# A decoder layer's opening: products of un-normed x, norms made beside them, and ten products of a constant ahead of all

## The chip, the cores and the metric

One core of a Trainium2 chip runs the whole layer. The metric is the time of one execution on the device in microseconds (us); lower is better. A core has five engines with programs of their own: TensorE (PE, matrix products), VectorE (DVE), ScalarE (ACT), GpSimd (POOL) and SyncE (SP), which here only issues loads and stores. Sixteen DMA engines move the data that SP, ScalarE and GpSimd ask for.

## What is computed

```
h   = RMSNorm_pre(x)                                   x: 512 tokens x 2048 channels, float32
[q | k | v | z_att | u | g_glu | z_conv] = h @ w_in    seven outputs of 1024 channels
group A: stick-breaking attention of q, k, v (8 heads x 128), times silu(z_att)
group B: GLU(u, g_glu) -> causal depthwise conv, 31 taps -> LayerNorm -> swish -> @ w_pw2, times silu(z_conv)
out = x + RMSNorm_post(concat(A, B) @ w_out)
RMSNorm_pre(x) = x * rsqrt(mean(x*x over the 2048 channels) + 1e-6) * g_pre
```

A token's root (the rsqrt) is one number for its whole row. A product may therefore be made from x times g_pre, or from x with g_pre multiplied into the weights, and its rows be scaled by the roots afterwards.

## The kernel before

Every float32 operand is split into a high and a low part in a shorter format (`split`: the high part by ScalarE, the low part by DVE), and a product is three products: high by high, high by low, low by high.

**The opening.** The first half of g_glu, 512 columns, is made ahead of everything else with x as the stationary operand. It runs in 16 blocks: the 2048 channels are four groups `kg` of 512, the 512 tokens four groups `m` of 128. A block (`rows_block`) is 12 products of 512 columns into the accumulator `gn` of its tokens; the four of one channel group share the weights `r_gn` of 1 MB, whose split is four calls of `part`. Ahead of a block its 128 x 512 piece of x is turned by four transposes (`turn_x`), split into `h_hi` and `h_lo`, and kept un-split as well (`keep_raw`). The blocks of channel group 0 use x un-normed, with g_pre in the weights (`g_col`). For groups 1 to 3 each piece of x is first normed on DVE (`scale_x`, by the root and by `g_bc`, the part of g_pre that TensorE spreads over all partitions, `broadcast_g`). The accumulators are brought to the same scale by `scale_up`. The squares for the roots are shared by ScalarE and DVE (`square`). At the end `norm_first` norms the turned pieces of group 0 again, since all later products need them normed.

**The order.** A table `plan` says what ScalarE and DVE do after each block; their programs and TensorE's stand as they are written. SP's and GpSimd's programs are laid out by a scheduler with priorities: `stream` gives the loads of later weights a high one. After the opening a list of steps follows, each with a load of 1 MB of weights and two units of 24 products: u in two halves of the channels (`u0`, first load named r_u01 for the second half of the channels, then r_u00), then q, k, v and so on. Between the units of the first step stand two groups of transposes: `turn_vectors`, which turns the taps and biases (`rows0`, `rows1`, loaded by `load_vectors`: 31 rows of taps and four single rows each, of 2 KB) into `vec`, and `turn_gates`, which turns the 512 columns of g_glu for the sigmoid.

**The buffers.** The raw weights have two buffers (`raws`), their high and low parts two each. A load of weights waits until the low parts of the weights two before it are made. SP's loads go round eight semaphores, so a load also waits for the landing of the eighth before it.

**The sums.** The v weights are used in sums and differences. GpSimd makes these in DRAM by 16 transfers of 1 MB (`vs`, `sum_next`): a copy, then a second one that adds to it. One is due after each block from the sixth on, then one after each unit; each adding transfer waits for its copy.

Of the kernel before, what the change touches and what calls it, by code (L numbers as in the profile page):

```python
# [16 lines left out]
P = 128  # L17
# [31 lines left out]
def hybrid_layer(  # L49
# [81 lines left out]
    pick = const.tile([4, 4, P], F32R, name="pick")  # L131
    for j in range(4):
        nc.gpsimd.tensor_copy(pick[:, j, :], ident[:4, j : j + 1].to_broadcast([4, P]))
# [15 lines left out]
    g_ks = early.tile([4, P], F32, name="g_ks")  # L149
    g_col = const.tile([P, 4], F32, name="g_col")  # L150
    g_rows = t2("g_rows")[:4]
    g_bc = {}

    def turn_g():

        ps = trp.tile([P, S], F32, tag="tr", name="g_col_ps")
        nc.tensor.transpose(ps[:, :4], g_ks, ident[:4, :4])
        nc.vector.tensor_copy(g_col, ps[:, :4])

    def split_g():  # L160
        g_parts = [t2(f"g_{part}", F32R)[:4] for part in ("hi", "lo")]
        split(*g_parts, g_rows)
        return g_parts

    def broadcast_g(j, g_hi, g_lo):

        ps = trp.tile([P, S], F32, tag="tr", name=f"g_ps{j}")
        nc.tensor.matmul(ps, pick[:, j, :], g_hi, start=True, stop=False)
        nc.tensor.matmul(ps, pick[:, j, :], g_lo, start=False, stop=True)
        g_bc[j] = t2(f"g_bc{j}")  # L170
        nc.vector.tensor_copy(g_bc[j], ps)
# [28 lines left out]

    def square(m, j, eng=None):
        junk = t2(f"junk{m}_{j}")
        total = sums[m][:, j : j + 1]
        if eng is None:
            nc.scalar.activation(junk, xts[m][j], AF.Square, accum_out=total)
        else:
            eng.tensor_tensor_reduce(
                out=junk, in0=xts[m][j], in1=xts[m][j], scale=1.0, scalar=0.0,
                op0=ALU.mult, op1=ALU.add, accum_out=total,
            )  # L210
# [3 lines left out]
    def root_table(m):  # L214
# [6 lines left out]
        rsqrt_table(y, v)  # L221
        roots[m] = y, v

# [15 lines left out]
    def turn_x(m, j):  # L239
# [9 lines left out]
        if j == 0:  # L249
            nc.scalar.copy(raw_h[m, 0], src)  # L250
        nc.vector.tensor_tensor(out=lo, in0=src, in1=f32(hi), op=ALU.subtract)

        def keep_raw():
            raw_h[m, j] = t2(f"xw{m}_{j}").rearrange("p (i t) -> p i t", i=4)
            nc.scalar.copy(raw_h[m, j], src)
# [21 lines left out]
    def norm_first():  # L277

        lo = {}
        for i in range(5):  # L280
            if i < 4:
                x, hi = whole[:, i, :], h_hi[0][:, i, :]
                nc.vector.scalar_tensor_tensor(
                    out=x, in0=x, scalar=g_col[:, i : i + 1], in1=rbc[0],
                    op0=ALU.mult, op1=ALU.mult,
                )
                nc.scalar.activation(hi, x, AF.Copy)
            if i > 0:
                nc.vector.tensor_tensor(
                    out=h_lo[0][:, i - 1, :], in0=whole[:, i - 1, :], in1=f32(h_hi[0][:, i - 1, :]),  # L290
                    op=ALU.subtract,
                )
            yield
# [39 lines left out]
    def pair(c0, post, name, halves=(0, 1)):  # L333
# [3 lines left out]
        def unit(half, i):  # L337
            def go(w):
                hi, lo = w
                if half == halves[0]:  # L340
                    ps[i] = mm(f"{name}_{i}")
                cs = slice(i * P, (i + 1) * P)
                for k in range(8):
                    mm3(
                        ps[i], (hi[:, k, cs], lo[:, k, cs]), h_at(half * 8 + k),
                        half == halves[0] and k == 0, half == halves[1] and k == 7,
                    )
                if half == halves[1]:
                    post(i, ps[i])
            return go  # L350

        for half in halves:
# [682 lines left out]
    with tc.manual_schedule(engines={mybir.EngineType.DVE, mybir.EngineType.Activation}):  # L1035
# [5 lines left out]
        def load_w0(kg, eng=nc.sync):  # L1041
            raw, hi, lo = (
                raws.tile([P, 4, S], F32, tag="raw", name=f"r_gn{kg}"),
                his.tile([P, 4, S], F32R, tag="hi", name=f"h_gn{kg}"),
                los.tile([P, 4, S], F32R, tag="lo", name=f"l_gn{kg}"),
            )
            w0[kg] = raw, hi, lo
            if kg == 0:
                for i in range(4):
                    eng.dma_start(raw[:, i], g_src(0)[i * P : (i + 1) * P, :])  # L1050
            else:
                eng.dma_start(raw, g_src(kg).rearrange("(k p) c -> p k c", p=P))

        def part(kg, i):
            raw, hi, lo = w0[kg]
            split(hi[:, i], lo[:, i], raw[:, i], g_col[:, i : i + 1] if kg == 0 else None)
# [11 lines left out]
        nc.sync.dma_start(g_ks, g_pre[: 4 * P].rearrange("(k p) -> k p", p=P))  # L1068
        load_x(0, 0)
        load_w0(0, nc.scalar)  # L1070
        nc.sync.dma_start(g_rows, g_pre.rearrange("(j c) -> j c", j=4))
        for m in range(1, NT):
            load_x(m, 0)
        load_x(0, 1, 2, 3)
        load_x(1, 1, 2, 3)
        load_w0(1)
        load_x(2, 1, 2, 3)
        load_x(3, 1, 2, 3)

        turn_g()  # L1080
        blocks = [(kg, m) for kg in range(4) for m in range(NT)]

# [10 lines left out]
        def do(f, *args):  # L1093
            return partial(f, *args)

        g_parts = []
        first = norm_first()
        keeps = {}

        plan = {  # L1100
            0: ([do(turn_block, 2)], [
                lambda: g_parts.extend(split_g()), do(square, 0, 1), do(square, 0, 2, dve),
                do(square, 0, 3),
            ]),
            1: ([do(turn_block, 3), lambda: broadcast_g(1, *g_parts)], [
                do(root_table, 0), do(square, 1, 1), do(square, 1, 2, dve), do(root, 0),
                do(square, 1, 3), do(root_table, 1), 
            ]),
            2: ([lambda: broadcast_g(2, *g_parts)], [
                do(scale_block, 4), do(part, 1, 0), do(scale_up, 0), do(root, 1),  # L1110
                do(scale_block, 5), do(part, 1, 1),
            ]),
            3: ([do(turn_block, 4), lambda: broadcast_g(3, *g_parts)], [
                do(square, 2, 1), do(part, 1, 2), do(square, 2, 2, dve), do(part, 1, 3),
                do(square, 2, 3), do(root_table, 2), do(scale_up, 1),
            ]),
            4: ([do(turn_block, 5)], [
                do(root, 2), do(scale_block, 6), do(square, 3, 1), do(square, 3, 2, dve),
                do(square, 3, 3), do(root_table, 3), do(scale_up, 2), do(load_w0, 2),
            ]),  # L1120
            5: ([do(turn_block, 6)], [
                do(root, 3), do(scale_block, 7), do(scale_up, 3), do(part, 2, 0), do(part, 2, 1),
            ]),
            6: ([do(turn_block, 7)], [do(scale_block, 8), do(part, 2, 2), do(part, 2, 3)]),
            7: ([do(turn_block, 8)], [do(scale_block, 9), do(scale_block, 10)]),
            8: ([do(turn_block, 9)], [do(load_w0, 3), do(scale_block, 11), do(part, 3, 0)]),
            9: ([do(turn_block, 10)], [do(scale_block, 12), do(part, 3, 1)]
                + [do(widen_root, m) for m in range(NT)]),
            10: ([do(turn_block, 11)], [
                load_vectors,  # L1130
                do(scale_block, 13), do(part, 3, 2), do(part, 3, 3)
            ]),
            11: ([do(turn_block, 12), broadcast_roots], [
                do(scale_block, 14)
            ]),
            12: ([do(turn_block, 13)], [
                do(scale_block, 15), lambda: loaded.update({0: steps[0].load()}),
            ]),
            13: ([do(turn_block, 14)], [do(keep_rows, 0)]),
            14: ([do(turn_block, 15)], [  # L1140
                do(keep_rows, 1), do(next, first)
            ]),
            15: ([], [do(next, first), do(keep_rows, 2), do(next, first)]),
        }
        loaded = {}
# [3 lines left out]
        turn_block(1)  # L1149
        for m in range(NT):  # L1150
            square(m, 0, dve)
        for n, (kg, m) in enumerate(blocks):
            if n < 4:
                for f in plan[n][0]:
                    f()
            rows_block(kg, m, ps0[m], w0[kg][1:], plan[n][0] if n >= 4 else ())
            for f in plan[n][1]:
                f()
            if 4 <= n + 1 < len(blocks):
# [4 lines left out]
        next(first)  # L1164
        next(first)
# [11 lines left out]

    heads_run = attention()
# [8 lines left out]
    for n, step in enumerate(steps):  # L1187
# [23 lines left out]
        if n + 1 < len(steps):  # L1211
# [43 lines left out]
```

## Time and profile before

| | |
|---|---|
| three runs, median (lowest to highest) | 878.05 us (875.48 to 878.66) |
| the profiled execution | 875.07 us |
| its span, first to last instruction | 873.4 us |
| mean granted TensorE clock | 0.995 |
| TensorE / VectorE / ScalarE / GpSimd busy | 98% / 72% / 45% / 14% of the span |
| moved by DMA | 163.32 MB, mean 187 GB/s |

The profile comes from one execution. Its page gives busy time by engine; the trace behind it answers by stretch (a table of busy time, granted clock and DMA share), by engine in order of time (with the idle time before an instruction and what ended it), and by group of instructions. In a row such as `PE L453 MATMUL gn<-h_gn,h_hi` the line is that of the kernel before, and names are without buffer numbers. A queue's issue is marked SPq or ACTq; it says when a load was asked for. When it landed is seen from who waited for it.

### The profile page before, as it was taken

How to read it: one execution, taken by the hardware profiler on the slowest of the kernel's cores; microseconds unless marked ns; L12 is line 12 of the kernel's file. 1: busy time of each engine (PE TensorE's matmuls, PEld its weight loads, DVE VectorE, ACT ScalarE, POOL GpSimd, SP SyncE). 2: the span in 40 equal slices, each digit the busy share in tenths (PEclk: the TensorE clock that was granted, in tenths of full speed). 3: DMA queues.
4: the chain of work that ended last, by engine and by line, in shares of the span. 5: the costliest groups of instructions: out<-in, count | busy, mean ns of one | idle time of the engine just before them, and what ended most of it. 6: DMA issues, size and time to landing. Idle time of an engine off the chain costs nothing.

```text
span 873.4 us, 9762 instructions
## 1 busy us (share of the span) xinstructions
PE 852.9 (98%) x3879; PEld 706.5 (81%) x3879; DVE 625.2 (72%) x742; ACT 392.3 (45%) x447; POOL 125.9 (14%) x157
## 2 busy tenths in 40 slices
PE   6899999999999999999999999999999999999995
PEld 4688888888888888888888888888888888888884
DVE  5766889996697978969696984235643776458775
ACT  5653424645443543343322545235722346455542
POOL 0012110001202132213111233032001000000032
PEclk9999999999999999999999999999999999999998
DMA  9499994558587565875497547862232246556782
GB/s 300 160 266 257 282 278 149 193 192 293 192 191 150 176 204 130 174 188 185 144 189 151 190 147 191 167 171 96 90 104 97 97 158 227 193 193 259 283 275 98
DMA packets 87262, 163.32 MB, mean 187 GB/s; under 512 B 2978, under 2 KB 52134, under 8 KB 83440
## 3 DMA queue, kind: packets, MB, share of 16 engines
q1 hardware_dynamic: 70320, 111.31, 37.6%
q0 software_dynamic: 16320, 50.33, 25.4%
q10 hardware_dynamic: 576, 1.05, 0.4%
q8 instruction: 30, 0.49, 0.2%
q14 instruction: 16, 0.13, 0.0%
HBM read 158.49 MB, written 54.53 MB: 244 GB/s over the span
## 4 chain that ended last, share of the span: by engine, by line
PE 87%; DVE 7%; ACT 2%; issue 2%; DMA 1%; DVEq 0%; SPq 0%; ACTq 0%
PE u L326 3%; PE u L328 3%; PE q L328 3%; PE u L327 3%; PE za L328 3%; PE zc L328 3%; PE q L327 3%; PE za L327 3%; PE zc L327 3%; PE za L326 3%; PE a L923 3%; PE q L326 3%; PE a L922 3%; PE zc L326 3%; PE a L924 3%; PE k L326 3%
## 5 line engine op out<-in xcount | busy, mean ns | idle before, releaser
L383 DVE SCALAR_TENSOR_TENSOR acc<-hg,vec,acc 128x512 f32<-128x512 f32 x240 | 182.3, 760 | 6.9
L100 DVE TENSOR_TENSOR l_w<-r_w,h_w 128x2048 fp32r<-128x2048 f32 x28 | 64.1, 2291 | 42.3 <-ACT h_w L99 42.3
L99 ACT ACTIVATE h_w<-r_w 128x2048 fp32r<-128x2048 f32 x28 | 53.5, 1915 | 43.6 <-DMA r_w<-ws 11.4
L326 PE MATMUL u<-h_hi,h_u 128*128 128x512 f32 x128 | 50.2, 392 | 0.0
L326 PE MATMUL q<-h_hi,h_q 128*128 128x512 f32 x128 | 50.1, 391 | 0.0
L326 PE MATMUL k<-h_hi,h_k 128*128 128x512 f32 x128 | 50.0, 391 | 0.0
L326 PE MATMUL za<-h_hi,h_za 128*128 128x512 f32 x128 | 49.9, 390 | 0.0
L328 PE MATMUL u<-h_hi,l_u 128*128 128x512 f32 x128 | 49.9, 390 | 0.0
L326 PE MATMUL zc<-h_hi,h_zc 128*128 128x512 f32 x128 | 49.9, 390 | 0.0
L328 PE MATMUL q<-h_hi,l_q 128*128 128x512 f32 x128 | 49.9, 390 | 0.0
L327 PE MATMUL u<-h_lo,h_u 128*128 128x512 f32 x128 | 49.9, 390 | 0.0
L327 PE MATMUL q<-h_lo,h_q 128*128 128x512 f32 x128 | 49.9, 390 | 0.0
L328 PE MATMUL za<-h_hi,l_za 128*128 128x512 f32 x128 | 49.8, 389 | 0.0
L327 PE MATMUL za<-h_lo,h_za 128*128 128x512 f32 x128 | 49.8, 389 | 0.0
L328 PE MATMUL zc<-h_hi,l_zc 128*128 128x512 f32 x128 | 49.8, 389 | 0.0
L328 PE MATMUL k<-h_hi,l_k 128*128 128x512 f32 x128 | 49.8, 389 | 0.0
L327 PE MATMUL k<-h_lo,h_k 128*128 128x512 f32 x128 | 49.8, 389 | 0.0
L327 PE MATMUL zc<-h_lo,h_zc 128*128 128x512 f32 x128 | 49.8, 389 | 0.0
L922 PE MATMUL a<-h_w,f_hi 128*128 128x512 f32 x128 | 49.8, 389 | 0.0
L923 PE MATMUL a<-l_w,f_hi 128*128 128x512 f32 x128 | 49.8, 389 | 0.0
L924 PE MATMUL a<-h_w,f_lo 128*128 128x512 f32 x128 | 49.8, 389 | 0.0
L653 POOL TENSOR_SCALAR_AFFINE_SELECT t<-t 128x128 f32<-128x128 f32 x64 | 35.7, 636 | 81.9 <-DVE t L676 48.9
(338 smaller groups left out, 2119.7 us busy)
## 6 DMA issues: line engine op xcount, KB each, us to landing
ws<-in_w_out_dram POOLq DMA_DIRECT2D x24, 1024.0 KB, 9.3
r_w<-ws SPq DMA_DIRECT2D x16, 1024.0 KB
vs<-in_w_in_dram POOLq DMA_DIRECT2D x12, 1024.0 KB, 13.8
r_w<-in_w_out_dram SPq DMA_DIRECT2D x12, 1024.0 KB
r_u<-in_w_in_dram SPq DMA_DIRECT2D x8, 1024.0 KB
r_q<-in_w_in_dram SPq DMA_DIRECT2D x8, 1024.0 KB
r_k<-in_w_in_dram SPq DMA_DIRECT2D x8, 1024.0 KB
r_v<-vs SPq DMA_DIRECT2D x8, 1024.0 KB
```

What stands on the lines that cost most here:

```text
L99: nc.scalar.activation(hi, src, AF.Copy)
L100: nc.vector.tensor_tensor(out=lo, in0=src, in1=f32(hi), op=ALU.subtract)
L326: nc.tensor.matmul(ps, wh, ah, start=first, stop=False)
L327: nc.tensor.matmul(ps, wh, al, start=False, stop=False)
L328: latest[0] = nc.tensor.matmul(ps, wl, ah, start=False, stop=last).ins
L383: bgq.append(lambda j=j: nc.vector.scalar_tensor_tensor(out=acc, in0=hg[:, j : j + S], scalar=vec[:, ct, j : j + 1], in1=acc, op0=ALU.mult ...
L653: nc.gpsimd.affine_select(out=blk, in_=blk, compare_op=ALU.is_gt, fill=0.0, base=0, pattern=[[-1, P]], channel_multiplier=1,)
L922: nc.tensor.matmul(ps, fh[:, kk, ts], hi[:, k, :], start=st, stop=False, skip_group_check=True)
L923: nc.tensor.matmul(ps, fh[:, kk, ts], lo[:, k, :], start=False, stop=False, skip_group_check=True)
L924: nc.tensor.matmul(ps, fl[:, kk, ts], hi[:, k, :], start=False, stop=en, skip_group_check=True)
```

## The change

- Groups 1 and 2 now use x un-normed too, with g_pre in the weights: `g_col` has 12 columns, and `part` scales for `kg < 3`. Only group 3 is normed by `scale_x`; its piece of g_pre is loaded spread out by SP (`load_g`), and `split_g`, `broadcast_g` and the tile `pick` are gone.
- `norm_first` now norms the turned pieces of three groups: 1 and 2 by tokens (four 128 x 128 passes a piece), 0 by channels, in the order 1, 0, 2, a norm, a high part and a low part a step.
- A turn stands inside the block ahead of its own; `scale_up` comes at blocks 9 to 12; the squares are shared out anew.
- SP's loads come in the order of use, the first weights among them; weights 2 and 3 are issued by GpSimd.
- Ten products of `mean_w`, a constant tile, into a tile that nothing reads stand first in TensorE's program.
- `turn_vectors` and `turn_gates` stand before the first step's units; u's first half is the first half of the channels, starting at channel group 1; the second step's weights are asked for before the loop.

```diff
-    g_ks = early.tile([4, P], F32, name="g_ks")
+    g_ks = early.tile([12, P], F32, name="g_ks")
...
+    def load_g(j):
+
+        g_bc[j] = t2(f"g_bc{j}")
+        nc.sync.dma_start(g_bc[j], g_pre[j * S : (j + 1) * S].partition_broadcast(P))
...
+        def by_tokens(j, m):
+            x, ts = raw_h[m, j], slice(m * P, (m + 1) * P)
+            for i in range(4):
+                norm(x[:, i, :], 4 * j + i, ts)
+            return h_hi[j][:, :, ts], h_lo[j][:, :, ts], x
...
+        todo = [(f, j, n) for j, f in ((1, by_tokens), (0, by_channels), (2, by_tokens)) for n in range(4)]
...
-        pair(C_U + t * 256, post_u(2 * t), f"u{t}", (0, 1) if t else (1, 0))
+        pair(C_U + t * 256, post_u(2 * t), f"u{t}")
...
+            k = kg * 4 + i
+            split(hi[:, i], lo[:, i], raw[:, i], g_col[:, k : k + 1] if kg < 3 else None)
...
+        nc.scalar.dma_start(g_ks, g_pre[: 12 * P].rearrange("(k p) -> k p", p=P))
         load_x(0, 0)
+        load_w0_rows(0)
+        load_w0_rows(1)
+        load_x(1, 0)
+        load_w0_rows(2)
+        load_w0_rows(3)
+        load_x(2, 0)
+        load_x(3, 0)
+        for m in range(NT):
+            load_x(m, 1)
         load_w0(1)
+        for m in range(NT):
+            load_x(m, 2, 3)
+        load_g(3)
+
+        idle = trp.tile([P, S], F32, tag="tr", name="idle")
+        for i in range(10):
+            nc.tensor.matmul(idle[:, :P], mean_w, mean_w, start=True, stop=True)
         turn_g()
...
+            3: [
+                do(load_w0, 2, nc.gpsimd), do(part, 1, 2), do(part, 1, 3),
+                do(square, 2, 1), do(square, 3, 1, dve),
+            ],
...
+            13: [lambda: loaded.update({0: steps[0].load()}), do(keep_rows, 0)],
+            14: [do(keep_rows, 1), do(next, first), do(next, first)],
+            15: [do(keep_rows, 2), do(next, first)],
...
         keep_rows(3)
-        next(first)
-        next(first)
+        for _ in range(4):
+            next(first)
+        loaded[1] = steps[1].load()
+        for _ in first:
+            pass
...
+    turn_vectors()
+    turn_gates()
     heads_run = attention()
...
-            if n == 0 and unit is step.units[-1]:
-                turn_gates()
-            if n == 0 and unit is step.units[0]:
-                turn_vectors()
```

Three places in the programs that this makes. The first is TensorE's, from the last block of the opening (gn3) to the first u products. Before:

```order
L328 MATMUL u0_0_732<-h_hi3_124,l_u01_639 128x512
L326 MATMUL u0_0_732<-h_hi3_124,h_u01_638 128x512
L327 MATMUL u0_0_732<-h_lo3_128,h_u01_638 128x512
L328 MATMUL u0_0_732<-h_hi3_124,l_u01_639 128x512
L191 MATMUL vec_ps_758<-ident_91,rows0_566 128x35 x4
L191 MATMUL vec_ps_758<-ident_91,rows1_572 128x35 x4
L326 MATMUL u0_1_768<-h_hi2_123,h_u01_638 128x512
L327 MATMUL u0_1_768<-h_lo2_127,h_u01_638 128x512
```

And with the change:

```order
L463 MATMUL gn3_138<-h_gn3_332,h_hi3_119 128x512
L464 MATMUL gn3_138<-l_gn3_333,h_hi3_119 128x512
L470 MATMUL gn3_138<-h_gn3_332,h_lo3_123 128x512 x4
L179 MATMUL vec_ps_745<-ident_91,rows0_575 128x35 x4
L179 MATMUL vec_ps_745<-ident_91,rows1_581 128x35 x4
L1188 MATMUL gT0_755<-ident_91,g_nat0_651 128x128
L1188 MATMUL gT0_755<-ident_91,g_nat1_676 128x128
L1188 MATMUL gT0_755<-ident_91,g_nat2_700 128x128
L1188 MATMUL gT0_755<-ident_91,g_nat3_706 128x128
```

The transposes of rows0 and rows1 stood behind the 24 products of u's first unit; now they stand right behind the last block, with the sixteen of the gates (gT0 to gT3) and then u's first product behind them.

The second is SP's program, from the first u load on. Before:

```order
L311 DMA r_u01_637<-in_w_in_dram 128x8x256
L184 DMA rows0_566<-in_conv_w_dram 31x512
L186 DMA rows0_566<-in_conv_b_dram 1x512
L186 DMA rows0_566<-in_ln_g_dram 1x512
L186 DMA rows0_566<-in_ln_b_dram 1x512
L186 DMA rows0_566<-in_b_pw2_dram 1x512
L184 DMA rows1_572<-in_conv_w_dram 31x512
L186 DMA rows1_572<-in_conv_b_dram 1x512
L186 DMA rows1_572<-in_ln_g_dram 1x512
L186 DMA rows1_572<-in_ln_b_dram 1x512
L186 DMA rows1_572<-in_b_pw2_dram 1x512
L311 DMA r_u00_726<-in_w_in_dram 128x8x256
```

And with the change:

```order
L319 DMA r_u00_645<-in_w_in_dram 128x8x256
L172 DMA rows0_575<-in_conv_w_dram 31x512
L174 DMA rows0_575<-in_conv_b_dram 1x512
L174 DMA rows0_575<-in_ln_g_dram 1x512
L174 DMA rows0_575<-in_ln_b_dram 1x512
L174 DMA rows0_575<-in_b_pw2_dram 1x512
L319 DMA r_u01_729<-in_w_in_dram 128x8x256
L172 DMA rows1_581<-in_conv_w_dram 31x512
L174 DMA rows1_581<-in_conv_b_dram 1x512
L174 DMA rows1_581<-in_ln_g_dram 1x512
L174 DMA rows1_581<-in_ln_b_dram 1x512
L174 DMA rows1_581<-in_b_pw2_dram 1x512
```

The five loads of rows1 stood ahead of the second u load; now they stand behind it.

The third is GpSimd's program, at the start of its transfers. Before:

```order
L137 CAST mean_w_103<-mean_f_101 128x128
L133 CAST pick_96<-ident_91 4x128 x4
L488 DMA vs500_433<-in_w_in_dram 512x1x512
L488 DMA vs501_461<-in_w_in_dram 512x1x512
L484 DMA vs500_433<-in_w_in_dram 512x1x512
```

And with the change:

```order
L134 CAST mean_w_98<-mean_f_96 128x128
L1057 DMA r_gn2_292<-in_w_in_dram 128x4x512
L1057 DMA r_gn3_331<-in_w_in_dram 128x4x512
L498 DMA vs500_368<-in_w_in_dram 512x1x512
L498 DMA vs501_409<-in_w_in_dram 512x1x512
L494 DMA vs500_368<-in_w_in_dram 512x1x512
```

The loads of weights 2 and 3 stand ahead of the first sums.

## Rows read from the trace of the kernel before

**Rows 1.** The page, busy time, share of the span and instructions of each engine.

```profile
PE 852.9 (98%) x3879; PEld 706.5 (81%) x3879; DVE 625.2 (72%) x742; ACT 392.3 (45%) x447; POOL 125.9 (14%) x157
```

**Rows 2.** Stretches: length, busy time of five engines, granted clock, DMA share, GB/s.

```profile
0.00:5.00 5.00, 0.24 (x1) 0.18 (x1) 0.16 (x1) 1.28 (x1) 2.04 (x14) 1.00 0.58 119
5.00:10.00 5.00, 2.62 (x10) 1.82 (x11) 1.75 (x3) 2.85 (x6) 0.00 (x0) 1.00 1.01 358
30.00:40.00 10.00, 7.72 (x36) 5.42 (x34) 6.91 (x19) 6.80 (x17) 0.88 (x1) 1.00 0.50 178
70.00:863.00 793.00, 792.85 (x3606) 660.02 (x3605) 572.81 (x635) 347.76 (x355) 115.12 (x136) 1.00 0.62 181
```

**Rows 3.** TensorE's timeline, first products: start us, duration us, line, out and inputs.

```profile
10.38 0.77 PE L453 MATMUL gn<-h_gn,h_hi 128*128 128x512 f32 x1
...
11.38 0.63 PE L453 MATMUL gn<-h_gn,h_hi 128*128 128x512 f32 x1
11.80 0.53 PE L454 MATMUL gn<-l_gn,h_hi 128*128 128x512 f32 x1
```

**Rows 4.** TensorE's timeline: starts of blocks, of u, the transposes, and q.

```profile
49.44 0.39 PE L453 MATMUL gn<-h_gn,h_hi 128*128 128x512 f32 x1
...
52.64 0.39 PE L453 MATMUL gn<-h_gn,h_hi 128*128 128x512 f32 x1
...
56.26 0.39 PE L453 MATMUL gn<-h_gn,h_hi 128*128 128x512 f32 x1
...
68.60 0.39 PE L326 MATMUL u<-h_hi,h_u 128*128 128x512 f32 x1
...
74.13 0.68 PE L191 MATMUL vec_ps<-ident,rows 35*128 35x35 f32 x8
...
80.33 1.91 PE L1174 MATMUL gT<-ident,g_nat 128*128 128x128 f32 x16
...
93.01 0.39 PE L326 MATMUL q<-h_hi,h_q 128*128 128x512 f32 x1
```

**Rows 5.** SP's timeline: when loads are issued, behind the opening's own.

```profile
41.31 0.37 SPq L311 DMA_DIRECT2D r_u<-in_w_in_dram  x1
...
48.82 0.22 SPq L186 DMA_DIRECT2D rows<-in_ln_g_dram  x1
54.66 0.22 SPq L186 DMA_DIRECT2D rows<-in_ln_b_dram  x1
...
56.43 0.39 SPq L311 DMA_DIRECT2D r_u<-in_w_in_dram  x1
62.10 16.50 SPq L311 DMA_DIRECT2D r_q<-in_w_in_dram  x2
```

**Rows 6.** SP's waits to 70 us: us in total, times, longest.

```profile
SPq L186 <- DMA rows<-in_conv_w_dram: 5.6, 1, 5.6
```

**Rows 7.** ScalarE's timeline: first use of two loads, idle time and its releaser.

```profile
73.97 1.92 ACT L99 ACTIVATE h_u<-r_u 128x2048 fp32r<-128x2048 f32 x1 [4.59 <-DMA r_u<-in_w_in_dram]
...
87.52 1.92 ACT L99 ACTIVATE h_q<-r_q 128x2048 fp32r<-128x2048 f32 x1 [9.03 <-DMA r_q<-in_w_in_dram]
```

**Rows 8.** GpSimd's timeline: an adding transfer of the sums, and its reader.

```profile
43.49 1.21 POOL L484 DMA_DIRECT2D vs<-in_w_in_dram  x1 [2.67 <-PE gn L460]
...
57.96 0.53 POOL L488 DMA_DIRECT2D vs<-vs  x1 [10.09 <-DMA vs<-in_w_in_dram]
```

**Rows 9.** Stretches as in rows 2: plain loads alone, and two adding transfers.

```profile
15.00:20.00 5.00, 3.96 (x16) 2.65 (x15) 4.25 (x15) 2.33 (x8) 0.00 (x0) 1.00 1.04 394
47.50:52.50 5.00, 5.00 (x26) 4.09 (x25) 3.84 (x10) 3.50 (x7) 0.37 (x1) 1.00 1.14 218
```

**Rows 10.** The same view, behind TensorE's last product.

```profile
865.00:870.00 5.00, 0.00 (x0) 0.00 (x0) 3.52 (x6) 0.72 (x1) 1.74 (x1) 0.54 0.55 186
```

**Rows 11.** Groups of instructions: busy us, mean ns, idle before. ScalarE's weight split, DVE's norm.

```profile
L102 ACT ACTIVATE h_gn<-r_gn,g_col 128x512 fp32r<-128x512 f32 x4 | 2.6, 721 | 0.0
L283 DVE SCALAR_TENSOR_TENSOR whole<-whole,g_col,rbc 128x512 f32<-128x512 f32 x4 | 2.9, 745 | 0.0
```

More of the change, by code (lines that the diff above doesn't have):

```diff
@@ L156, in turn_g @@
         ps = trp.tile([P, S], F32, tag="tr", name="g_col_ps")
[L157 to L169, printed above, removed]
+        nc.tensor.transpose(ps[:, :12], g_ks, ident[:12, :12])
+        nc.vector.tensor_copy(g_col, ps[:, :12])
+    def load_g(j):
         g_bc[j] = t2(f"g_bc{j}")
-        nc.vector.tensor_copy(g_bc[j], ps)
+        nc.sync.dma_start(g_bc[j], g_pre[j * S : (j + 1) * S].partition_broadcast(P))
     NV = TAPS + 4
@@ L220, in root_table @@
         )
-        rsqrt_table(y, v)
         roots[m] = y, v
+    def root_table(m):
+        rsqrt_table(*roots[m])
     def root(m):
@@ L277, in norm_first, with norm, by_channels @@
     def norm_first():
[L279 to L286, printed above, removed]
-                nc.scalar.activation(hi, x, AF.Copy)
[L288 to L292, printed above, removed]
+        def norm(x, i, ts):
+            nc.vector.scalar_tensor_tensor(
+                out=x, in0=x, scalar=g_col[:, i : i + 1], in1=rbc[0][:, ts],
+                op0=ALU.mult, op1=ALU.mult,
+            )
+        def by_tokens(j, m):
[3 more added lines that the diff above has]
+            return h_hi[j][:, :, ts], h_lo[j][:, :, ts], x
+        def by_channels(j, i):
+            x = whole[:, i, :]
+            norm(x, i, slice(0, S))
+            return h_hi[j][:, i, :], h_lo[j][:, i, :], x
+        todo = [(f, j, n) for j, f in ((1, by_tokens), (0, by_channels), (2, by_tokens)) for n in range(4)]
+        made = []
+        for n in range(len(todo) + 2):
+            if n < len(todo):
+                f, j, i = todo[n]
+                made.append(f(j, i))
+            if 1 <= n <= len(todo):
+                hi, _, x = made[n - 1]
+                nc.scalar.activation(hi, x, AF.Copy)
+            if n >= 2:
+                hi, lo, x = made[n - 2]
+                nc.vector.tensor_tensor(out=lo, in0=x, in1=f32(hi), op=ALU.subtract)
             yield
@@ L1094, in do @@
             return partial(f, *args)
-        g_parts = []
         first = norm_first()
-        keeps = {}
+        loaded = {}
         plan = {
[L1101 to L1129, printed above, removed]
-                load_vectors,
[L1131 to L1143, printed above, removed]
@@ new lines, in hybrid_layer @@
+            5: [
+                do(square, 2, 2), do(square, 2, 3, dve), do(root_table, 0), do(square, 3, 2),
+                do(square, 3, 3, dve), do(root_sum, 1),
+            ],
+            6: [
+                do(part, 2, 0), do(root_table, 1), do(root, 0), do(part, 2, 1), do(root_sum, 2),
+                do(root_sum, 3),
+            ],
+            7: [
+                do(part, 2, 2), do(root_table, 2), do(root, 1), do(part, 2, 3), do(root_table, 3),
+            ],
+            8: [do(part, 3, 0), do(root, 2), do(root, 3)]
+                + [do(widen_root, m) for m in range(NT)],
@@ new lines, in hybrid_layer @@
+            9: [
+                do(part, 3, 1), broadcast_roots, do(scale_block, 12), do(scale_up, 0),
+            ],
+            10: [do(part, 3, 2), do(scale_block, 13), do(scale_up, 1), do(next, first)],
+            11: [
+                do(part, 3, 3), do(scale_block, 14), do(scale_up, 2), do(next, first),
+                load_vectors,
+            ],
+            12: [do(scale_block, 15), do(next, first), do(scale_up, 3), do(next, first)],
+            13: [lambda: loaded.update({0: steps[0].load()}), do(keep_rows, 0)],
@@ L1148, in hybrid_layer @@
             part(0, i)
-        turn_block(1)
-        for m in range(NT):
-            square(m, 0, dve)
+        keeps[0]()
         for n, (kg, m) in enumerate(blocks):
[L1153 to L1157, printed above, removed]
+            rows_block(
+                kg, m, ps0[m], w0[kg][1:], [do(turn_block, n + 1)] if n + 1 < len(blocks) else ()
+            )
+            for f in plan[n]:
                 f()
-            if 4 <= n + 1 < len(blocks):
+            if n + 1 < len(blocks):
                 keeps[n + 1]()
@@ L1210, in hybrid_layer @@
             sum_next(sumq)
-        if n + 1 < len(steps):
+        if n + 1 < len(steps) and n + 1 not in loaded:
             loaded[n + 1] = steps[n + 1].load()
```

79 lines of the change are left out of this document (39 added, 40 removed).

## Prediction

> **What bounds the kernel now.** I read the page first, for the engine that is full [rows 1]: TensorE is busy for 98% of the span. The table by stretch tells where the other 2% lie [rows 2]: 792.85 of 793 us from 70 to 863 are busy, so behind the opening every microsecond that TensorE starts earlier or later reaches the end one for one, as long as its operands are there. TensorE is idle in the opening (0.24 of the first 5 us busy, 2.62 of the next 5, 7.72 of 10 from 30 to 40). The opening is therefore what the change can shorten, and what follows it must not become late. The timeline of TensorE gives the prices there [rows 3, 4]: a block of the first gate product with its turn takes 3.20 us when nothing is waited for (49.44 to 52.64), one with four more transposes 3.62 (to 56.26). The first product starts at 10.38, the u products at 68.60, q at 93.01. The 24.41 us from u to q hold 96 products, the eight transposes of the vectors (at 74.13) and the sixteen of the gates (at 80.33).
>
> The second thing to see is the DMA behind the opening, read from SP's own timeline, its waits and ScalarE's [rows 5 to 7]. Second-half u weights are issued at 56.43 and ScalarE gets them at 73.97: 17.5 us for 1 MB. The first q weights are issued from 62.10 and come at 87.52: 25.4 us, 13.55 behind the u weights ahead of them. The first u load took 7.5 (41.31 to 48.82). What makes the difference is GpSimd's sums of the v weights [rows 8]: the accumulating load of 43.49 had landed only when its reader was let go at 57.96, and while these run the engines are full (1.14) at 218 GB/s, against 394 for plain loads [rows 9].
>
> **The change, part by part.**
>
> *Head of TensorE's program.* Ten 128-column products come before the first transposes. The early products show half rate (11.38 to 11.80 is 0.42 us for 512 columns, [rows 3]), so ten of 128 cost at least 1.1 us and, if each cost as much as a 512-column one, 4.2. I take 2 to 3: nothing else is due there, since x has to land first. They end near 4.7, and x's first turn follows. Zero on the path, up to 1 if they run long.
>
> *Loads of the opening.* Block 0 needs its x, four weight rows and block 1's x, six loads of 262 KB (1.57 MB), now first in SP's queue. 119 GB/s to 5 us and 358 behind [rows 2] have moved that much by 7.7. ScalarE then has one split of x and four of weights at 0.72 [rows 11], 3.6 us from 6.0; the last low part, one DVE pass of 0.75, is ready at 10.3, TensorE has five products left, and block 1 starts at 11.4. Weights 2 now go through GpSimd's queue and share the engines with weights 1; I charge 0.8 (0 if they just arrive, 3.2, a block, if not).
>
> *Blocks 1 to 15.* No norm lies between load and turn any more, so the pace is TensorE's own. 14 blocks at 3.20 give 44.8, the last without a turn 2.78 (3.20 less 0.42), the broadcast of the roots 0.42, the charge 0.8: the last product ends at 11.4 + 44.8 + 2.78 + 0.42 + 0.8 = 60.2, against 68.60. The six products that broadcast g go with the stalls they are in. ScalarE and DVE can follow: their fullest stretch is blocks 10 to 15, where DVE has some 3 to 4.5 us a block for norm, low part and splits (0.75 a pass, four token-wise quarter passes together between 0.75 and 3.0, about 1 taken), and late low parts have two blocks of slack. Bounds for 60.2: 59.4 without the charge, 68.6 if new stalls eat it all.
>
> *What stands between that and u.* The vector and gate transposes now stand ahead of u, not among its products. They cost the same, so u to q stays 24.41. But their cover is gone. In the kernel before, the vectors' second half (rows1) was issued before the second u load and had till 74.13. Now SP's program has rows1 behind the second u load (r_u01), and TensorE asks for it at 60.2. Every later product is queued behind these transposes.
>
> *When rows1 lands.* r_u01 needs the buffer of weights 3, free when their last low part is made, 0.4 behind the start of block 12: 11.4 + 11 x 3.20 + 0.42 + 0.8 + 0.4 = 48.2 (the kernel before: block 12 at 56.26, issue at 56.43). From there two legs. First r_u01: 17.5 us if it fares like the second u load, 25.4 if like the q load [rows 5, 7]. I take 25.4: as it is issued, the first u load, issued near 37 beside the first accumulating sums and not ahead of them, is itself still on its way, and the next four sums come while it waits; that is what lay around the q load. Then rows1 behind it: 5.8, as the first rows behind the first u load (48.82 to 54.66, a wait of 5.6 on the 62 KB of taps, [rows 5, 6]), or 13.55, as q behind u. So rows1 lands at 48.2 + 25.4 + 5.8 = 79.4 to 87.2; I take 81.5, nearer the small load. Low bound 48.2 + 17.5 + 5.8 = 71.5; lower still, with 7.5 for r_u01, 61.5.
>
> 62 KB for 5.6 us is odd beside 1 MB in 7.5, by bytes it should be 0.5; the row decides, and 5.8 stays in the sum. The Trainium skill (DMA: Bandwidth & Descriptors, on why a DMA increments its semaphore by 16) says how many of the 16 engines carry a load: the largest number up to 16 that divides the outer dimension, so 31 rows go to one. The trace agrees with 5.6 us; spread over all engines rows1 would be 5 us sooner and my sum 5 us less.
>
> *The restart.* After 21 us without a product the clock is down: granted 0.54 in the stretch behind the last product [rows 10]. 24 transposes and the first u products then run at half rate: 1 to 5 us, 2.5 taken.
>
> *Nothing else on the path.* Squares move among engines with slack; scale_x of three quarters goes, norm_first takes its place behind the roots; ScalarE's and DVE's later norm passes queue behind the gates and vec, but by the same prices finish some 12 us after rows1, while u's second half starts 16 after it. GpSimd's two weight loads stand ahead of the sums, which wait for block 5 anyway. The q load comes 5 to 14 behind rows1, before u ends.
>
> **Sum.** q starts at 81.5 + 24.41 + 2.5 = 108.4 against 93.01: +15.4 us, on the profiled execution's 875.07 that is 890.5. The runs' median, 878.05, lies 3 above that execution, so the median I expect is 893.
>
> **Rivals.**
> 1. *The vectors are there in time.* The place is the same one wait; it decides at 60.2. r_u01 and rows1 would need to land in 12 us together. For it: 7.5 for the first u load, and the sums might be slower to start. Against: that load went just ahead of the accumulating sums, and neither later load did better than 17.5. Then the opening's 8.4 us are kept: 878.05 - 8.4, some 869.5.
> 2. *A short wait.* r_u01 takes 17.5, rows1 5.8: 71.5 + 24.41 + 2.5 - 93.01 = +5.4, 883.5. With rows1 at 66 gain and wait cancel; from 61.7 to 70.5 no difference can be told.
> 3. *The opening itself does not get faster* (weights late, ScalarE behind), without a wait on the vectors: 878. With that wait it costs little more, for the wait covers it.
>
> **How the numbers follow.** Long wait 0.62, short wait 0.18, no wait 0.17, no effect 0.03. A measurement here tells 0.5%, 4.4 us, from no change. Faster: nearly all of rival 1 and a trace of 2, 0.18. Same: most of rival 2's shorter half and rival 3, 0.13. Slower: the long wait and the rest of 2, 0.69. The long wait alone spans 886 (restart 1, rows1 at 76) to 902 (rows1 at 87.2, restart 5). The range that holds 8 in 10 reaches from there through rival 2 to the edge of rival 1: 869 to 902.
>
> **What would show it.** Right: TensorE's last gate product ends near 60; the largest wait on TensorE is the vectors' transposes on the load of rows (taps or a small row), some 20 us; ScalarE's sigmoid and DVE's copy of vec stand behind it; a dip of the granted clock there; q near 108, and from q to the end the same time as before. Each step alone: block 1 near 11.4; blocks 3.2 apart; the second u load issued near 48. Wrong: no such wait, u within 3 us of the last gate product (rival 1); rows landed before 72 (rival 2); or gaps between the blocks (rival 3).

## The result

| | kernel before | changed kernel |
|---|---|---|
| median of 18 runs each (lowest to highest) | 878.76 us (874.75 to 882.58) | 881.01 us (879.15 to 883.87) |
| profiled execution | 875.07 us | 881.33 us |
| its span | 873.4 us | 879.6 us |
| start of q's first product | 93.01 | 99.46 |
| mean granted TensorE clock | 0.995 | 0.989 |

The changed kernel takes 1.0038 times the time of the kernel before (95% interval 1.0022 to 1.0054): a little slower, some 3 us, inside the 0.5% that the prediction counted as no change. The forecast was 893 with a range of 869 to 902. The sign and the mechanism came out; the size did not. The executions of the kernel before fall into two groups, 48 of the 93 on record between 874.6 and 875.7 us and 45 between 877.5 and 882.6, and 12 of the 18 here are of the second, so its median is no steady mark (875.0 to 878.8 on record) and the ratio, which rests on all executions, is what counts.

### The profile page after: what moved, and what is told of

It is laid out like the page before. It is cut to its first block, busy times and chain, and to the rows that moved or that the text cites. A ratio compares the mean times of both kernels' runs of the same rounds, so it can differ in the third digit from the quotient of the medians.

```text
span 879.6 us, 9809 instructions
## 1 busy us (share of the span) xinstructions
PE 855.4 (97%) x3883; PEld 711.3 (81%) x3883; DVE 630.8 (72%) x770; ACT 396.4 (45%) x454; POOL 126.2 (14%) x155
## 4 chain that ended last, share of the span: by engine, by line
PE 94%; DMA 4%; DVE 1%; ACT 0%; issue 0%; SPq 0%; DVEq 0%
PE u L336 3%; PE u L334 3%; PE u L335 3%; PE q L336 3%; PE k L334 3%; PE za L334 3%; PE zc L334 3%; PE k L335 3%; PE za L336 3%; PE q L334 3%; PE a L932 3%; PE zc L336 3%; PE q L335 3%; PE k L336 3%; PE za L335 3%; PE a L934 3%
## 5 line engine op out<-in xcount | busy, mean ns | idle before, releaser
L663 POOL TENSOR_SCALAR_AFFINE_SELECT t<-t 128x128 f32<-128x128 f32 x64 | 35.6, 635 | 81.1 <-DVE t L686 48.2
```

The lines of the kernel that those rows point to most:

```text
L663: nc.gpsimd.affine_select(out=blk, in_=blk, compare_op=ALU.is_gt, fill=0.0, base=0, pattern=[[-1, P]], channel_multiplier=1,)
```

## The profile after

The page's busy times, to set beside [rows 1]:

```profile
PE 855.4 (97%) x3883; PEld 711.3 (81%) x3883; DVE 630.8 (72%) x770; ACT 396.4 (45%) x454; POOL 126.2 (14%) x155
```

TensorE has 2.5 us more of busy time than before for much the same products, and still the span is 6.2 us longer: it stands still somewhere, and somewhere it runs slower. TensorE's waits over the first 140 us, all of them (us in total, times, longest):

```profile
PE vec_ps L179 <- DMA rows<-in_b_pw_dram: 10.5, 1, 10.5
PE idle L1101 <- POOL mean_w L134: 1.8, 1, 1.8
PE gn L463 <- ACT h_gn L102: 1.3, 1, 1.3
PE xT L237 <- DMA x<-in_x_dram: 0.7, 1, 0.7
```

There is one large wait, at the place that the prediction named: the transposes of rows1, held by a small row that goes the same way as the taps. TensorE's timeline has the rest (start us, us; the starts of blocks 1 and 2 of the opening come first; [rows 4] are the same places before):

```profile
13.77 0.40 PE L463 MATMUL gn<-h_gn,h_hi 128*128 128x512 f32 x1
...
17.00 0.39 PE L463 MATMUL gn<-h_gn,h_hi 128*128 128x512 f32 x1
...
61.06 1.07 PE L470 MATMUL gn<-h_gn,h_lo 128*128 128x512 f32 x4
62.06 0.43 PE L179 MATMUL vec_ps<-ident,rows 35*128 35x35 f32 x4
72.97 0.61 PE L179 MATMUL vec_ps<-ident,rows 35*128 35x35 f32 x4 [10.47 <-DMA rows<-in_b_pw_dram]
73.51 3.67 PE L1188 MATMUL gT<-ident,g_nat 128*128 128x128 f32 x16
76.84 0.78 PE L334 MATMUL u<-h_hi,h_u 128*128 128x512 f32 x1
...
99.46 0.39 PE L334 MATMUL q<-h_hi,h_q 128*128 128x512 f32 x1
```

Three terms can be read off. The last gate product ends, and the vectors are asked for, at 62.06, where the kernel before came to u at 68.60: -6.54 us. The wait: +10.47. And 99.46 - 62.06 - 10.47 = 26.93 us for the transposes and the 96 u products that took 24.41 before: +2.52. The sum is +6.45, which is q's shift (99.46 - 93.01). The +2.52 is TensorE at half rate behind the wait, the restart. From q's start to the last product it is 769.8 us, against 770.1 before. So all that the change does is done by q.

The stretches behind the last gate product (columns as in [rows 2]) show the clock's two levels, 2.4 GHz (1.00) and 1.2 GHz (0.50):

```profile
63.00:65.00 2.00, 0.00 (x0) 0.00 (x0) 2.00 (x4) 1.98 (x3) 0.62 (x1) 0.94 1.10 219
65.00:67.00 2.00, 0.00 (x0) 0.00 (x0) 2.00 (x7) 0.31 (x1) 2.00 (x3) 0.50 1.08 223
...
77.00:78.00 1.00, 1.00 (x4) 0.81 (x4) 1.00 (x4) 1.00 (x3) 0.00 (x0) 0.50 1.03 408
```

TensorE stood still from 62.5, and when it started again at 72.97 the granted clock was 0.50, and stayed there until 78: the gates' sixteen transposes took 3.67 us in place of 1.91 [rows 4].

What rows1 waited for is on SP's timeline (issues) and in the view of DMA issues (KB each, us from issue to landing; the first line is that of the 1 MB issued at 49.78, the second that of the adding transfer issued at 58.96):

```profile
49.78 0.40 SPq L319 DMA_DIRECT2D r_u<-in_w_in_dram  x1
50.23 0.43 SPq L172 DMA_DIRECT2D rows<-in_conv_w_dram  x1
...
58.55 0.22 SPq L174 DMA_DIRECT2D rows<-in_b_pw_dram  x1
```

```profile
r_u<-in_w_in_dram SPq DMA_DIRECT2D x1, 1024.0 KB, 11.4
vs<-in_w_in_dram POOLq DMA_DIRECT2D x1, 1024.0 KB, 13.2
```

The second u load landed at 49.78 + 11.4 = 61.2, before TensorE asked for anything. The 70 KB of rows1 (62 of taps, four rows of 2) behind it needed until 72.97, another 11.8 us. Beside them ran adding transfers of the v sums, issued at 58.96 and 64.38.

The trace also records the start of each DMA packet; a row of taps or of a bias is one packet of 2 KB, and behind the opening SP's queue has 70 of this size, 35 for rows0 and 35 for rows1. Those of rows1 start one after another, all but the first between 63.40 and 72.07, most of them 0.25 us apart.

## The experiments

The changed kernel's own time, 881.01, and its ratio, 1.0038, are the base line; every run gives its ratio to executions of the kernel before on the same chip.

**1. Both rows earlier.**

```diff
         load_g(3)
+        load_vectors()
...
                 do(part, 3, 3), do(scale_block, 14), do(scale_up, 2), do(next, first),
-                load_vectors,
```

> Edit: the ten loads of rows0 and rows1 are asked for right behind the opening's own loads, ahead of both u loads. Theory (the order of the loads makes the wait): rows1 is there long before TensorE asks, so the 10.5 us wait and the half-rate restart behind it (gates 3.67 for 1.91 us, u's first products some 0.7) go; u starts near 62.1 + 0.7 + 1.9 = 64.7 in place of 76.84 and the time falls by up to 12 us, to 869. Rival A (the next load is late): TensorE stops at u's second half or at q instead, since those weights were issued at 49.8 and 59.6 and stay where they are; then 872 to 878, with a wait of 3 to 9 us on the h_u or h_q of that load. Rival B (the taps crowd the opening's loads): blocks 4 or 8 start later than 26.7 or 39.5 and the last gate product ends later than 62.

Measured: 870.19 us, ratio 0.9921 (0.9892 to 0.9949). TensorE has no wait on rows or on u; the rows of its timeline:

```profile
61.77 0.68 PE L179 MATMUL vec_ps<-ident,rows 35*128 35x35 f32 x8
...
63.25 1.64 PE L1188 MATMUL gT<-ident,g_nat 128*128 128x128 f32 x13 [0.31 <-ACT g_nat L1077]
64.64 0.48 PE L334 MATMUL u<-h_hi,h_u 128*128 128x512 f32 x1
...
86.50 0.39 PE L334 MATMUL q<-h_hi,h_q 128*128 128x512 f32 x1
```

u starts at 64.64 (64.7 expected), q 6.5 us ahead of the kernel before. Neither rival shows: no wait at u's second half or q, and the last gate product ends where it did. With the loads in this order the wait (10.5) and its restart (2.5) are gone together, the 13 us between q at 99.46 and q at 86.50. This kernel is faster than the changed one and than the one before.

**2. The same place, another shape.**

```diff
-            nc.sync.dma_start(rows[half][0:TAPS], conv_w.rearrange("k o c -> (k o) c")[:, cs])
+            taps = conv_w.rearrange("k o c -> (k o) c")[:, cs]
+            nc.sync.dma_start(rows[half][0:16], taps[0:16])
+            nc.sync.dma_start(rows[half][16:TAPS], taps[16:TAPS])
```

> Edit: the 31 rows of taps are loaded as 16 and 15 rows, in the same place, behind the second u load. Theory (one engine carries 31 rows, and there they take turns with the adding sums' packets): the second u load lands at some 61, the taps just behind it, rows1 by 62 to 65; the wait of TensorE falls from 10.5 to 0 to 3 us, and so does the half rate; time 869 to 873. SP's wait on rows<-conv_w (4.6 us) goes. Rival (rows1 is late because it stands behind 1 MB in the queue, in whatever shape): the wait stays at 8 us or more, time 879 to 881.

Measured: 870.23 us, ratio 0.9921 (0.9891 to 0.9950). The view of DMA issues, for the second u load (issued at 49.59) and the two pieces of taps behind it (50.51 and 52.40):

```profile
r_u<-in_w_in_dram SPq DMA_DIRECT2D x1, 1024.0 KB, 11.9
...
rows<-in_conv_w_dram SPq DMA_DIRECT2D x1, 32.0 KB, 11.2
rows<-in_conv_w_dram SPq DMA_DIRECT2D x1, 30.0 KB, 9.4
```

They land at 61.5, 61.7 and 61.8. Behind the same load, with adding transfers issued at 57.02 and 61.92, the same taps come 0.3 us after it, where rows1 took 11.8, and TensorE waits for nothing at the vectors (vec at 61.87, u at 64.71). The edit splits the taps of rows0 as well; the second u load behind them lands at 61.5 against 61.2, so that part made no difference to it. The Trainium skill (DMA: Bandwidth & Descriptors, on why a DMA increments its semaphore by 16) puts a load on the largest number of engines up to 16 that divides its outer dimension, which is one for 31 rows, 16 for 16 and 15 for 15: these landings agree.

**3. The sums later.**

```diff
-            if n >= 5:
+            if n >= 13:
                 sum_next(v_sumq)
```

> Edit: the sums of the v weights begin behind block 13 in place of block 5; nothing else moves. Theory (adding transfers slow the loads beside them): with none on the way between 37 and 56, both u loads land within 8 us and rows1 before 62; no wait of TensorE on rows, last gate product at 62, u near 64.7; the time falls by 8 to 12, to 869 to 873, unless the sums now come too late for the v products, which would show as a wait on r_v and take 2 to 10 us back. Rival (the order in SP's queue alone makes the wait): rows1 still lands near 73, time 881.

Measured: 875.25 us, ratio 0.9987 (0.9969 to 1.0004). The second u load now takes

```profile
r_u<-in_w_in_dram SPq DMA_DIRECT2D x1, 1024.0 KB, 4.9
```

and vec, gates and u follow without a wait (vec 61.25, u 64.12, q 85.98). So the wait goes once more, with place and shape untouched. The 35 packets of rows1 still start one after another, from 53.20 to 56.26, but 0.08 us apart in place of 0.25. While they run, the DMA share is that of one engine in sixteen (columns as in [rows 2]):

```profile
54.50:55.50 1.00, 1.00 (x6) 0.80 (x5) 1.00 (x3) 1.00 (x2) 0.00 (x0) 1.00 0.06 25
```

But the sums are then late, as the expectation allowed. TensorE's waits from 100 to 200 us:

```profile
PE vc L626 <- ACT h_v L99: 3.7, 1, 3.7
PE vc L627 <- DVE l_v L100: 1.5, 1, 1.5
```

with a granted clock of 0.74 from 150 to 160; from q to the end it is 777.2 us, 7 more than in the kernel before, and the time is the same as that kernel's within the interval.

Each of the three edits removes the wait alone. It takes all three circumstances together: rows1 behind the second u load, its taps as one load of 31 rows, and the adding transfers on the way.

**4. The transposes where they were.**

```diff
-    turn_vectors()
-    turn_gates()
...
+            if n == 0 and unit is step.units[-1]:
+                turn_gates()
+            if n == 0 and unit is step.units[0]:
+                turn_vectors()
```

> Edit: the transposes of the vectors and of the gates go back to where they were, behind u's first and second units; the loads stay. Theory (rows1 lands near 73 whatever TensorE does): TensorE asks for rows1 at 62.1 + 5.5 = 67.5 and waits some 5.4 us in place of 10.5, the half rate behind it shorter; time 881 - 5 - 1 to 2 = 874 to 875, about the kernel before. Rival (what TensorE waits for moves with it, the landing being set by work that TensorE's progress lets go): the wait stays near 10, time 880.

Measured: 875.25 us, ratio 0.9982 (0.9964 to 1.0000). The timeline, from the transposes on:

```profile
68.69 0.43 PE L179 MATMUL vec_ps<-ident,rows 35*128 35x35 f32 x4
72.10 0.61 PE L179 MATMUL vec_ps<-ident,rows 35*128 35x35 f32 x4 [2.98 <-DMA rows<-in_b_pw_dram]
72.64 0.79 PE L334 MATMUL u<-h_hi,h_u 128*128 128x512 f32 x1
...
76.65 0.59 PE L334 MATMUL u<-h_hi,h_u 128*128 128x512 f32 x1
77.07 0.41 PE L335 MATMUL u<-h_lo,h_u 128*128 128x512 f32 x1
```

rows1 comes at 72.10, about when it did, so the rival falls; TensorE, with a unit of u done first (and 1.1 us of it spent waiting for low parts of `norm_first`), asks at 69.1 in place of the expected 67.5 and waits 3.0. In this shorter stop too the clock fell, and ten products ran some 0.43 us apart behind it. The stretches (columns as in [rows 2]):

```profile
70.00:71.00 1.00, 0.00 (x0) 0.00 (x0) 1.00 (x2) 0.42 (x1) 0.00 (x0) 0.62 1.10 227
71.00:72.00 1.00, 0.00 (x0) 0.00 (x0) 1.00 (x1) 0.00 (x0) 0.00 (x0) 0.50 1.15 238
```

**5. The wait filled.** The time of the wait is given to products that nothing reads.

```diff
         for c in range(CT):
+            for _ in range(46 if c == 4 else 0):
+                nc.tensor.matmul(hot, mean_w, h_hi[3][:, 0], start=True, stop=True)
             nc.tensor.transpose(
```

> Edit: on the changed kernel, 46 products of 512 columns into a tile that nothing reads stand between the transposes of rows0 and those of rows1, some 10.4 us, as long as the wait there. The wait for rows1 stays and its time is filled. Theory (the wait costs twice: 10.5 us of standing, and a half rate behind it of 1.8 on the gates' transposes and 0.7 on u's first products): gates 1.91 us again, u's products 0.23 from the first on, time 881 - 2.5 = 878.5. Rival (the gates and u are slow there for another cause, such as their operands): they stay slow, time 881 or, if the filling runs over the landing, more.

Measured: 878.78 us, ratio 1.0022 (1.0005 to 1.0039).

```profile
62.09 11.00 PE L181 MATMUL hot<-h_hi,mean_w 128*128 128x512 f32 x46
73.02 0.43 PE L182 MATMUL vec_ps<-ident,rows 35*128 35x35 f32 x4
73.39 1.97 PE L1191 MATMUL gT<-ident,g_nat 128*128 128x128 f32 x16
75.11 0.47 PE L337 MATMUL u<-h_hi,h_u 128*128 128x512 f32 x1
...
96.98 0.39 PE L337 MATMUL q<-h_hi,h_q 128*128 128x512 f32 x1
```

The filling ends where the wait did (73.02 for 72.97), and rows1 came no earlier: its last packet starts at 72.22 (72.07 in the changed kernel). The gates take 1.97 and u starts at full rate. From the transposes of rows1 to q it is 23.96 us in place of 26.49: the restart, 2.53, by itself. The rows show this, the times do not yet: the ratio falls from 1.0038 to 1.0022, and the two intervals overlap.

**6. The move alone, on the kernel before.** `turn_vectors` and `turn_gates` ahead of u, all else as it was.

```diff
+    turn_vectors()
+    turn_gates()
     heads_run = attention()
...
-            if n == 0 and unit is step.units[-1]:
-                turn_gates()
-            if n == 0 and unit is step.units[0]:
-                turn_vectors()
```

> Edit: on the kernel before, the transposes of the vectors and of the gates alone go ahead of u, as the change has them; the opening and the loads stay. Theory (the move costs only by the load it meets, and rows1 stands ahead of the second u load here): rows1 is there at 68.6 or comes within 3 us, u's start moves from 68.6 to 72 to 74, q's from 93.0 to 93 to 95, time 875 to 877. Rival (the move itself costs, as nothing covers rows1's landing in any order of the loads): rows1 lands near 74, a wait of 4 to 6 us and a half rate behind it, time 880 to 883.

Measured: 876.26 us, ratio 0.9997 (0.9976 to 1.0017). No wait: `vec` at 68.73 for 0.68 us, gates at 69.34, u at 71.06, q at 92.94 (93.01 before). The move is free where rows1 stands ahead of the second u load; the last packet of rows1 starts at 66.56 there, 2.2 us before TensorE asks.

**7. The ten products.** They are taken out of the kernel of experiment 1 (early_noidle) and out of the changed kernel (no_idle), and put into the kernel before (before_idle); in early_warm twelve more of them go into the gaps of TensorE's first 7 us in the kernel of experiment 1. The edit of early_noidle, against experiment 1:

```diff
-        idle = trp.tile([P, S], F32, tag="tr", name="idle")
-        for i in range(10):
-            nc.tensor.matmul(idle[:, :P], mean_w, mean_w, start=True, stop=True)
```

> Edit: on the kernel with both rows loaded early, the ten products of the constant tile are taken out. Theory (they stand where TensorE waits for x and end before it is there): nothing moves, x's first turn at 5.0, block 1 at 13.8, time as with them, 870.2 within 0.5. Rival (they keep TensorE's clock up): block 1 starts later, at 14.2 to 15, and the time is 0.5 to 1.2 us longer.

> Edit: on the kernel with both rows loaded early, twelve more products of the constant tile are added, four behind the turn of g and eight behind the first turn of x, so that TensorE has work in the gaps at 4.4 to 5.0 and 6.1 to 7.4. Theory (block 0 runs at half rate, 0.43 us a product to 13.3, because TensorE stood still in those gaps): products reach 0.23 us before 10, block 1 starts at 11.4 to 12.3 as the prediction had it, the time falls by 1.5 to 2.4 us, to 868 to 869. Rival (block 0 waits for ScalarE's and DVE's splits of the first weights, or the rate rises at a fixed time): block 1 stays at 13.8, time 870.

> Edit: the ten products of the constant tile alone are taken out of the changed kernel. Theory (they raise no rate; with them block 0 was at half rate to 11.8 to 13.4 in seven profiles, without them to 10.5 in one): full rate by 11, block 1 at 12.3 to 12.8 in place of 13.8, the last gate product a microsecond earlier, and no gain in the end, since rows1 still lands near 73: 880 to 881. Rival (the moment of the rise varies by itself, as between the kernel before, 11.9, and the same opening with the turns moved, 13.2): block 1 at 13.0 to 13.8; time 881 as well.

> Edit: the ten products of the constant tile alone are put at the head of TensorE's program in the kernel before. Theory (they bring nothing): the opening's waits for x, the squares and the norms stay, full rate between 11.9 and 13.4, time the same within 0.3%. Rival A (they raise the clock early): full rate before 11, time 1 us less. Rival B (they put the rise off): full rate later than 13.4, 1 us more.

Measured, with the ratio to the kernel before: early_noidle 869.80 us, 0.9920 (0.9896 to 0.9944); early_warm 870.98, 0.9925 (0.9902 to 0.9949); no_idle 880.54, 1.0035 (1.0017 to 1.0053); before_idle 878.00, 1.0008 (0.9987 to 1.0029). None differs clear of noise from its partner (0.9921, 0.9921, 1.0038, 1). What varies is the moment at which products go from 0.43 us to 0.23. Without the products, in early_noidle and then in no_idle:

```profile
10.88 0.39 PE L464 MATMUL gn<-l_gn,h_hi 128*128 128x512 f32 x1
...
12.47 0.39 PE L463 MATMUL gn<-h_gn,h_hi 128*128 128x512 f32 x1
```

```profile
10.94 0.63 PE L464 MATMUL gn<-l_gn,h_hi 128*128 128x512 f32 x1
...
13.75 0.39 PE L463 MATMUL gn<-h_gn,h_hi 128*128 128x512 f32 x1
```

The same head of TensorE's program, 10.9 against 13 or later. So my reading of one profile, that the products put the rise off, fell with the second. In the kernel before the rise comes near 12 without the products and near 14.3 with them (before_idle), but also at 13.3 without them in experiment 6: profiles of one execution each do not settle whether the products move it. early_warm, in which TensorE had work almost without a gap from 1.77 on, still has products at 0.43 us up to 12.40 and block 1 at 13.85: filling the gaps did not bring the rise forward either.

**8. rows1 by another queue.** ScalarE issues the five loads of rows1.

```diff
+            eng = nc.scalar if half else nc.sync
-            nc.sync.dma_start(rows[half][0:TAPS], conv_w.rearrange("k o c -> (k o) c")[:, cs])
+            eng.dma_start(rows[half][0:TAPS], conv_w.rearrange("k o c -> (k o) c")[:, cs])
...
-                nc.sync.dma_start(rows[half][i : i + 1], src[None, cs])
+                eng.dma_start(rows[half][i : i + 1], src[None, cs])
```

> Edit: the five loads of rows1 are issued by ScalarE, at the same place of the plan (near 52 us), in place of SP behind the second u load; the 31 rows stay one load. Theory (rows1 is late by two things: its place in SP's queue behind a load that itself lands at 61, and then 31 rows one after the other beside an adding transfer, some 9 to 12 us): without the first, rows1 lands near 52 + 10 = 62, the wait falls from 10.5 to 0 to 3, time 869 to 873. Rival (the one engine's work in sum sets the landing, in whatever queue): rows1 lands at 70 or later, wait 8 or more, time 879 to 881.

Measured: 881.57 us, ratio 1.0046 (1.0024 to 1.0069). The time does not answer the question. ScalarE's issues, and TensorE's wait:

```profile
48.10 0.63 ACT L298 ACTIVATE h_hi<-xw 128x512 fp32r<-128x512 f32 x1
55.52 0.23 ACTq L175 DMA_DIRECT2D rows<-in_ln_g_dram  x1
...
58.55 0.23 ACTq L175 DMA_DIRECT2D rows<-in_b_pw_dram  x1
58.83 0.59 ACT L248 COPY xw<-xT 128x512 f32<-128x512 f32 x1 [10.09 <-DMA rows<-in_ln_b_dram]
```

```profile
PE gn L464 <- ACT h_hi L242: 7.9, 1, 7.9
```

The loads wait for earlier landings, as SP's do [rows 6]; on ScalarE that wait holds everything behind it. The opening itself stood still for 7.9 us, and rows1 was there when it was over at 70.66. The packets answer instead: those of rows1 start between 51.27 and 62.90 on ScalarE's queue, so rows1 came near 63, about where the theory has it, and not at 70 or later.

## Why the prediction was right or wrong

*The wait and its place: right.* One wait, on rows1, at the first transposes behind the last gate product, with the restart behind it. Experiments 1 to 3 remove it three ways, and each time q starts 12.9 to 13.5 us earlier.

*The first leg: the step that failed.* "First r_u01: 17.5 us if it fares like the second u load, 25.4 if like the q load [...] I take 25.4." It took 11.4. The reason given for 25.4 did not hold: the first u load was not still on its way (its last packet starts at 47.55, and the second load is issued at 49.78), and in place of four sums one older adding transfer ran until 55.9 (15.9 from its issue at 40.01), a copy was issued at 56.47 and an adding transfer at 58.96. Both rows that I chose between were late by their last packets. In the kernel before, 960 of the second u load's 1024 packets had started by 64, and the other sixteenth only by 73.66, behind the rows of rows0 and rows1, which go one by one from 47.62 to 67.95. The last packets of the q load then start 0.21 us apart from 73.85 to about 87, beside two adding transfers. The 7.5 of the first u load, which I set aside as the lucky one, was nearer. Alone this leg is worth 14 us of the forecast.

*The second leg: too short.* "Then rows1 behind it: 5.8 [...] or 13.55." It took 11.8, inside these bounds. The 5.8 was no price for all of rows1: ten rows of rows0 had started before the first u load landed at 48.82, and it ends with the taps, ahead of the four single rows. Adding transfers were on the way there too, and the rows went at the same 0.25 us apart. In the changed kernel one row of rows1 starts at 60.90, the next at 63.40, the last tap at 70.58 and the last single row at 72.07. The two errors, -14.0 and +6.0, and an issue 1.6 later (49.78 for 48.2) bring 79.4 to 73.0, where rows1 came; the forecast had rounded 79.4 up to 81.5. The sentence that spreading would save 5 us was right in kind and too small: it saved all of the wait, 10.5.

*The restart: right.* 2.5 us were taken; 2.52 came out of the trace and 2.53 out of experiment 5. The bounds were 1 to 5 and the stop was half as long as forecast, so that the middle was hit is partly luck.

*The opening: nearly.* 60.2 forecast, 62.06 measured. Blocks are 3.22 us apart (3.20), and the charge of 0.8 for weights 1 was not paid: 13.77 + 14 x 3.22 + 2.78 + 0.42 = 62.05. The difference is block 1, at 13.77 and not 11.4: I had five products of block 0 left at 10.3 and priced them at full rate; eight were left, and they ran at half to 13.

*The ten products at nothing: right*, in time, by four runs; they took 2.40 us where TensorE had nothing else to do.

*From span to median: wrong.* I added 3 us because the runs' median lay 3 above the profiled execution. But that median had the second group of executions in it, near 879, and the profile was of the first. Two kernels with the same opening (experiment 6, and before_idle) were profiled at 880.08 and 877.95: q starts at 92.94 and 93.12, but then TensorE waits for the k weights (3.0 and 2.1 us), and experiment 6 ends its last product at 868.1 in place of 863.1. This may be what the second group of the kernel before has; no profile of it there is on record. The changed kernel's profiled execution, 881.33, is already at its median. So between profiled executions the change costs 6.3 us, between medians 2.3, and by the ratio 3.3.

With 11.4 and 11.8 for the two legs and nothing added at the end, the sum would have been 48.2 + 11.4 + 11.8 + 24.41 + 2.5 - 93.01 = +5.3, or 880.4, beside the 881.33 of the profiled execution. That is rival 2, the short wait, whose 883.5 was given 0.18; its two legs, 17.5 and 5.8, are wrong one by one and right in sum (23.3 for 23.2), which is luck.

## What to carry to other kernels

When a step loses its cover, look at the place of its smallest load in the queue, and at the number of its rows, before anything else: 70 KB behind 1 MB and beside adding transfers cost 13 us here, and moving the issue, or splitting 31 rows into 16 and 15, gave 1.2% over the changed kernel and 0.8% over the one before. A landing time borrowed from another load carries that load's neighbours with it, so it is not taken at the upper end of its bounds unless a row says that the neighbours are the same. And a median above the profiled execution belongs to that kernel and its mix of executions; it is not an offset to add to its successor.

## What the runs showed of the chip

- The granted clock fell from 1.00 to 0.50 in a stop of 2.98 us (experiment 4; shorter waits of 1.1 us in all came just before it), and ten products of 512 columns ran at some 0.43 us before it was back.
- At the program's start products run at half rate in stretches whose granted clock is 1.00. In the changed kernel, by TensorE's timeline and by stretch:

```profile
11.82 0.63 PE L464 MATMUL gn<-l_gn,h_hi 128*128 128x512 f32 x1
12.25 1.69 PE L470 MATMUL gn<-h_gn,h_lo 128*128 128x512 f32 x4
```

```profile
12.00:13.00 1.00, 1.00 (x4) 0.81 (x3) 0.00 (x0) 0.00 (x0) 0.00 (x0) 1.00 1.04 383
```

  That first rise came between 10.9 and 14.3 in the profiles here, at different times for the same head of TensorE's program, and in early_warm work put in front of it did not bring it forward.
- rows1 behind the same 1 MB: 11.8 us with its taps as one load of 31 rows; as 16 and 15 rows the taps came 0.3 us behind it.
- The rows of a load of 31 start one after another: 0.08 us apart with no adding transfer on the way (experiment 3), 0.25 beside one (the changed kernel, and the kernel before).
- A load of 1 MB can wait for its last sixteenth: in the kernel before 960 of the 1024 packets of the second u load had started by 64 us, the last at 73.66, and ScalarE got the load at 73.97.
